# A two-block kernel: x also loaded transposed, weight units laid out in order of use, recurrence gates issued sooner, values with tokens on partitions, and the last norm's gain on VectorE

## The chip, the cores and the metric

The kernel runs on one core of a Trainium2 chip. The metric is device time of one execution in microseconds. Engines are named as the profile does: PE is TensorE's matmuls, PEld its weight loads, DVE is VectorE, ACT ScalarE, POOL GpSimd, SP SyncE. SPq and ACTq are the queues in which SyncE and ScalarE issue DMAs.

## The reference, cut to what matters

Two blocks follow one another on x of 512 tokens by 1024 features, in float32.

```
# first block
h = rmsnorm(x, norm1_g);  p = h @ w_in                    # 1024 -> 512 lru_x | 512 lru_gate | 512 four_in
c = centred_depthwise_conv(lru_x, conv_w, conv_b)         # width 4 along tokens
for direction in (forward, backward):
    r, i = sigmoid(c @ w_a + b_a), sigmoid(c @ w_x + b_x) # blocks of 64 x 64
    a = exp(8 r log_sigmoid(lam));  h_t = a h_{t-1} + sqrt(1 - a^2) (i c)
x = x + concat(gelu(lru_gate) * (h_f + h_b), fourier_mix(four_in)) @ w_out
x = x + expert_choice_moe(rmsnorm(x, norm2_g))            # 16 experts, 64 tokens each, 1024 -> 2048 -> 1024
x = rmsnorm(x, normf_g)
# second block
q, k, v, z_a, u, z_s, g_a, g_s = split(rms_norm(x, norm_gain) @ w_in_2)
y_a = (band_attention(q, k, v, rel_bias) * silu(z_a)) @ w_attn_out      # 8 heads; rel_bias by distance
y_s = gelu(s5_ssm(u));  y_s = glu(y_s @ w_glu) * silu(z_s) @ w_ssm_out  # complex state space, 32 groups
x = x + (sigmoid(g_a) * y_a + sigmoid(g_s) * y_s) @ w_out_2
return rms_norm(x, final_gain)
```

## The kernel before

Every engine executes the instructions in the order in which the program issues them to it; nothing reorders them. The tile framework adds the waits between engines. A buffer of a pool is used again once its last readers are done.

**Precision.** Matmuls of the two blocks run on a pair of a rounded part and a rest: `Pair.put` copies the rounded part on ScalarE (L106, or L109 with a scale) and subtracts it on VectorE or GpSimd (L107, L110), and `mm3` does three matmuls for a product (L120 to L122), so a unit of eight feature blocks is 24 matmuls of 128x512.

**Weights.** `Stream` loads units of 128x1024 floats (512 KB) on SyncE's queue into two buffers of two units each, `work` splits a unit and issues the next load, and `get` hands out a split unit and keeps about two ahead. A unit of w_in is 128 columns of it, read in pieces of 128 floats for each row of the matrix. Of three splits one subtracts on VectorE and two on GpSimd.

**Head.** Four blocks of 128 tokens of x are loaded (L253), transposed on TensorE into eight PSUM banks (L319) and split into `hT` with the norm's gain (L324). The squares for the norm run on ScalarE (L283), and the log-sigmoid chain of the recurrences runs on VectorE (L294 to L315). Two units are projected as hT arrives; `inv_sqrt` (L218 to L229), four scaled identities and one matmul make `rr`, the norm's scale of each token in every partition (L349). Four projections feed the convolution: for each block b one multiplication by rr (L373), one scaled copy on ScalarE (L374), three steps on VectorE (L378), and a split. `gates(b)` does the four gate products of a block with four sigmoids on ScalarE (L366); block 0's stand in the loop at b == 3, after the work on the third block. Then come the fourier projections (L426 to L432), the decays (`decay`, L398 to L401) and recurrences (`recur`, L405 to L411), pumped in between the gelu projections, the channel and token products of the Fourier mix (L453 to L476), and the output projection.

**Middle.** Router and expert choice, then 16 experts whose weights stream through two rings of buffers on SyncE's queue (`prefetch`, L201). The tables of the state space are made beside them.

**Second block.** `proj` projects one unit, tokens along the free dimension. After the queries and keys and the chunk scans of the state space come the four units of the values: `values(b)` projects 128 value columns and multiplies them by rr (L1280), and `turn_values(b)` transposes them by four matmuls (L1286) and copies them into `vt`, tokens on partitions (L1287). They stand in this order: values 0, chunk outputs 0 to 2 (L1262, L1263), turn 0, values 1, chunk outputs 3, the four turned outputs (L1271, copied into `Yc`, L1272), turn 1; then the write of Yc to DRAM (L1309), the load of the bias table `bt` on ScalarE's queue into the buffer of `U`, which the chunk outputs read (L1312), a subtraction and a fill of it on GpSimd (L1313, L1314), a fill of the two key tiles `kl` on GpSimd (L1319), and the split of head 0; then values 2, values 3, turn 2, the score matmuls of head 0 (L1370, and L1371, which reads `kl`), and turn 3. From there `fill` places 24 projections among the eight heads.

**Tail.** After the last output projection each half of a token block gets the residual (L1520), a square on ScalarE (L1523) and a multiplication by the gain on GpSimd, the very last half on VectorE (L1524); `finish` makes the scale in small VectorE steps (L218 to L229) and applies it half on ScalarE, half on VectorE (L1500, L1503).

Of the kernel before, what the change touches and what calls it, by code (L numbers as in the profile page):

```python
# [16 lines left out]
OP = mybir.AluOpType  # L17
# [35 lines left out]

NRING = 3
# [5 lines left out]
def body(ctx, tc, a, out, dbg=None):  # L60
# [63 lines left out]
    class Stream:  # L124
# [6 lines left out]
        def load(self, n=1):  # L131
            for _ in range(n):
                if self.units:
                    if self.half is None:
                        pair = wr.tile([128, 2, 1024], F32, name="w", tag="w")
                        t, self.half = pair[:, 0], pair[:, 1]
                    else:
                        t, self.half = self.half, None
                    for src, shape, *sub in self.units.pop(0):
                        v = t.rearrange(shape[0], **shape[1]) if shape else t  # L140
                        SP.dma_start(v[:, :, sub[0], :] if sub else v, src)
                    self.loaded.append(t)
# [18 lines left out]

    def cols_unit(w, c0, k=DB, width=128):

        return [(w[:, c0:c0 + width].rearrange("(k p) c -> p k c", p=128), ("p (k c) -> p k c", {"k": k}))]

    def rows_unit(w, k):
        return [(w[k * 128:(k + 1) * 128, :], None)]
# [68 lines left out]
    with ExitStack() as c1:  # L236
# [5 lines left out]
        with ExitStack() as ca:  # L242
# [5 lines left out]
            ws = Stream([cols_unit(a["w_in"], b * 128) for b in (0, 1, 2, 3, 8, 9, 10, 11, 4, 5, 6, 7)] +  # L248
                        [rows_unit(a["w_out"], k) for k in (4, 5, 6, 7, 0, 1, 2, 3)])
            for tb in range(TB):  # L250
                if tb == TB - 1:
                    ws.load()
                SP.dma_start(xs[:, tb, :], a["x"][tb * 128:(tb + 1) * 128, :])  # L253
                if tb == 0:
                    SP.dma_start(cst, a["cst"][:, 0:CCK])
                    SP.dma_start(pp, a["pp"])
            ws.load(3)
# [12 lines left out]
            ps = [bank() for _ in range(DB)]  # L270
# [11 lines left out]
            def squares(tb):  # L282
                act(h2n[:, tb, :], xs[:, tb, :], AF.Square, accum_out=ss[:, tb:tb + 1])  # L283
# [33 lines left out]
            for tb in range(TB):  # L317
                for d in range(DB):
                    PE.transpose(ps[d][:, tb * 128:(tb + 1) * 128], xs[:, tb, d * 128:(d + 1) * 128], ident)  # L319
                if 0 < tb < TB - 1:  # L320
                    squares(tb)
            ws.work(DVE)
            for d in range(DB):
                hT.put((slice(None), d), ps[d], DVE, scale=P("n1", d, d + 1))  # L324
                if d == 1:
                    ws.work(POOL)
            squares(TB - 1)
# [9 lines left out]

            w = [ws.done.pop(0) for _ in range(2)]
            two = [bank(), bank()]
            for k, i in [(k, i) for j in (range(3), range(3, DB)) for i in range(2) for k in j]:  # L340
                mm3(two[i], w[i][:, k * 128:(k + 1) * 128], hT[:, k, :], start=(k == 0), stop=(k == DB - 1))
            inv_sqrt(ta, ss, "n1", rt)
            dg = early2[:, 1]
            for tb in range(TB):
                DVE.tensor_scalar(dg[:, tb * 128:(tb + 1) * 128], ident, rt[:, tb:tb + 1], None, op0=OP.mult)
# [4 lines left out]

            two.append(in_proj())

# [18 lines left out]
            for b in range(5):  # L371
                if b < 4:
# [61 lines left out]
            fourier(0, pf)  # L434
# [5 lines left out]
            for g in range(1, 4):  # L440
                fourier(g, in_proj())
# [425 lines left out]
    order = [4, 0, 1, 2, 3, 5, 6, 7, 8, 9]  # L867
    units = [cols_unit(a["w_in_2"], g * 512 + b * 128) for g in order for b in range(4)]
    units += [cols_unit(a["w_attn_out_2"], b * 256, 4, 256) for b in range(4)]
    for b in range(4):  # L870
        units.append([(a["w_glu_2"][:, j * 512 + b * 128:j * 512 + b * 128 + 128].rearrange("(k p) c -> p k c", p=128),
                       ("p (k j c) -> p k j c", {"k": 4, "j": 2}), j) for j in range(2)])
    units += [cols_unit(a["w_ssm_out_2"], b * 256, 4, 256) for b in range(4)]
    units += [rows_unit(a["w_out_2"], k) for k in range(DB)]
    ws = Stream(units)
# [399 lines left out]
    vT = {}  # L1275

    def values(b):
        p = proj()
        vT[b] = scratch("vT")
        DVE.tensor_tensor(vT[b], p, rr, op=OP.mult)  # L1280

    def turn_values(b):
        t = vT.pop(b)
        p = bank()
        for tb in range(TB):
            PE.transpose(p[:, tb * 128:(tb + 1) * 128], t[:, tb * 128:(tb + 1) * 128], ident)  # L1286
        act(vt[:, :, b * 128:(b + 1) * 128], p.rearrange("p (t c) -> p t c", t=TB), AF.Copy)  # L1287
# [45 lines left out]
    values(2)  # L1333
    values(3)
    turn_values(2)
# [287 lines left out]
```

## Time and profile before

| | us |
|---|---|
| median of 3 runs (1524.46 to 1530.74) | 1527.55 |
| profiled execution | 1526.82 |
| its span, first to last instruction | 1525.0 |
| TensorE matmuls busy in the span | 1458.1 (96%) |
| VectorE, ScalarE, GpSimd busy | 609.8, 401.3, 192.2 |
| HBM read | 453.16 MB |

The profile is of one execution. Times in its rows count from the first instruction. An instruction's row gives its start, how long it was busy, engine and line, what it writes and reads, and in square brackets how long its engine was idle before it and which instruction or DMA ended that. Matmuls overlap, so the distance between two starts tells more than a duration.

### The profile page before, as it was taken

To read this page: it belongs to the slowest core of one execution; us is meant where nothing else is said; L and a number is where in the kernel's file an instruction comes from. 1 tells how busy PE (TensorE), PEld (TensorE's weight loads), DVE (VectorE), ACT (ScalarE), POOL (GpSimd) and SP (SyncE) were. 2 spreads that over 40 slices of the span, in tenths; PEclk is the share of its full clock that TensorE was granted. 3 is DMA by queue.
4 is the path that set the end of the run, shared out by engine and by line. 5 is a ranking of instruction groups with operands and counts; after the bars stand their busy time and mean duration, and the time that the engine had idled before them with its cause. 6 is when DMAs were issued, how large, how long until landed. Compare 5 with 4: busy or idle time off the path is not lost.

```text
span 1525.0 us, 17325 instructions
## 1 busy us (share of the span) xinstructions
PE 1458.1 (96%) x6856; PEld 807.0 (53%) x6856; DVE 609.8 (40%) x1278; ACT 401.3 (26%) x688; POOL 192.2 (13%) x128
## 2 busy tenths in 40 slices
PE   8899899999999999999999999899999899999997
PEld 6678633333333334443334343343478787777885
DVE  6773512221222244333342323442253745554454
ACT  5744211100100210100100100111173156664533
POOL 3423000000001000000000001000022232212353
PEclk9999899999999999999999999999999999999999
DMA  6116979999999999999999999999947152223331
GB/s 223 56 55 272 372 326 411 427 427 425 427 426 411 425 425 427 428 426 426 427 426 425 427 427 422 396 420 427 387 126 139 56 138 63 76 83 105 99 114 55
DMA packets 141345, 459.67 MB, mean 301 GB/s; under 512 B 16654, under 2 KB 87694, under 8 KB 93008
## 3 DMA queue, kind: packets, MB, share of 16 engines
q1 hardware_dynamic: 138848, 454.23, 74.8%
q10 hardware_dynamic: 1760, 2.62, 0.5%
q0 software_dynamic: 656, 1.71, 0.4%
q8 instruction: 54, 0.88, 0.2%
q14 instruction: 27, 0.22, 0.0%
HBM read 453.16 MB, written 4.19 MB: 300 GB/s over the span
## 4 chain that ended last, share of the span: by engine, by line
PE 78%; DMA 9%; DVE 6%; ACT 3%; issue 2%; POOL 1%; SPq 0%; ACTq 0%; POOLq 0%; DVEq 0%
PE gu L1058 25%; PE dn L1081 13%; DMA w<-in_w_up_dram 8%; PE ps L122 8%; PE ps L120 8%; PE ps L121 8%; PE tp L920 4%; PE tp L956 3%; PE tp L1045 2%; PE dn L1104 1%; DVE cT L378 1%; PE tp L945 1%; PE ps L1406 1%; ACT sh L1038 1%; PE ps L1394 1%
## 5 line engine op out<-in xcount | busy, mean ns | idle before, releaser
L1058 PE MATMUL gu<-w,xT 128*64 128x512 f32 x2032 | 472.0, 598 | 11.4 <-DMA w<-in_w_up_dram 10.6
L1058 PEld LDWEIGHTS gu<-w,xT 128*64 128x64 f32 x2032 | 167.7, 137 | 279.0 <-issue 228.6
L1081 PE MATMUL dn<-w,sh 128*64 128x512 f32 x944 | 218.0, 599 | 0.0
L958 DVE TENSOR_TENSOR xs<-tp,xs 128x512 f32<-128x512 f32 x120 | 77.5, 686 | 279.3 <-PE tp L956 279.3
L120 PE MATMUL ps<-hTh,w 128*128 128x512 f32 x416 | 167.2, 402 | 2.3 <-DVE early L475 1.5
L122 PE MATMUL ps<-hTh,w 128*128 128x512 f32 x416 | 165.2, 397 | 0.6 <-POOL w L107 0.6
L121 PE MATMUL ps<-hTl,w 128*128 128x512 f32 x416 | 165.1, 397 | 0.2 <-DVE hTl L110 0.2
L107 POOL TENSOR_TENSOR w<-w 128x1024 fp32r<-128x1024 f32 x51 | 124.1, 2436 | 279.1 <-ACT w L106 266.5
L1081 PEld LDWEIGHTS dn<-w,sh 128*64 128x64 f32 x944 | 63.9, 137 | 116.0 <-issue 115.3
L1038 ACT ACTIVATE sh<-gu 128x512 f32<-128x512 f32 x32 | 19.1, 597 | 396.1 <-PE gu L1058 393.8
L106 ACT ACTIVATE w<-w 128x1024 fp32r<-128x1024 f32 x80 | 83.7, 1054 | 64.6 <-PE ps L122 41.3
L120 PEld LDWEIGHTS ps<-hTh,w 128*128 128x128 f32 x416 | 78.9, 190 | 22.1 <-issue 3.5
L122 PEld LDWEIGHTS ps<-hTh,w 128*128 128x128 f32 x416 | 78.8, 189 | 19.7 <-POOL w L107 1.3
L121 PEld LDWEIGHTS ps<-hTl,w 128*128 128x128 f32 x416 | 78.8, 189 | 18.6 <-DVE hTl L110 0.6
L956 PE MATMUL tp<-Y,GT 128*128 128x512 f32 x240 | 72.3, 421 | 0.4 <-ACT ssm_BM L838 0.4
L956 PEld LDWEIGHTS tp<-Y,GT 128*128 128x128 f32 x240 | 40.1, 188 | 52.0 <-issue 44.6
L1040 DVE COPY sh<-gu 128x512 f32<-128x512 f32 x32 | 22.1, 690 | 103.8 <-PE gu L1058 69.6
L107 DVE TENSOR_TENSOR w<-w 128x1024 fp32r<-128x1024 f32 x29 | 41.8, 1445 | 51.8 <-ACT w L106 51.8
L849 POOL DMA_DIRECT2D ssm_BM<-raw x8 | 4.2, 536 | 459.5 <-DVE raw L845 459.5
L925 ACT ACTIVATE xin<-tp 128x512 f32<-128x512 f32 x16 | 9.6, 597 | 189.7 <-PE tp L920 189.7
L931 DVE TENSOR_TENSOR xT<-tp,pp 128x512 f32<-128x512 f32 x16 | 11.1, 692 | 117.6 <-PE tp L929 117.6
L1045 PE MATMUL tp<-cst,sh 128*128 128x128 f32 x256 | 39.1, 287 | 17.4 <-DVE sh L1053 11.7
(446 smaller groups left out, 1726.9 us busy)
## 6 DMA issues: line engine op xcount, KB each, us to landing
w<-in_w_gate_dram SPq DMA_DIRECT2D x127, 1024.0 KB, 13.3
w<-in_w_up_dram SPq DMA_DIRECT2D x127, 1024.0 KB, 14.3
w<-in_w_down_dram SPq DMA_DIRECT2D x118, 1024.0 KB, 14.7
w<-in_w_in_dram SPq DMA_DIRECT2D x52, 512.0 KB, 4.8
w<-in_w_out_dram SPq DMA_DIRECT2D x16, 512.0 KB, 4.3
w<-in_w_down_dram SPq DMA_DIRECT2D x16, 512.0 KB, 8.0
xs<-in_x_dram SPq DMA_DIRECT2D x4, 512.0 KB, 5.5
h2n<-in_w_down_dram SPq DMA_DIRECT2D x2, 1024.0 KB, 19.0
```

Of the source, the lines that this page charges most:

```text
L106: act(h, src, AF.Copy)
L107: eng.tensor_tensor(l, src, h.bitcast(F32), op=OP.subtract)
L120: PE.matmul(p, x[0], y[0], start=start, stop=False)
L121: PE.matmul(p, x[0], y[1], start=False, stop=False)
L122: PE.matmul(p, x[1], y[0], start=False, stop=stop)
L920: PE.matmul(p[h * 64:h * 64 + 64], G[:, tb, :], src[:, tb, h * 512:(h + 1) * 512], start=(tb == 0), stop=(tb == TB - 1))
L956: PE.matmul(p, GT[e][:, tb * 128:(tb + 1) * 128], Yt[e][h * 512, 512][i], start=(i == 0), stop=(i == 1))
L958: DVE.tensor_add(sl, p, sl)
L1038: act(o, i, AF.Copy)
L1045: PE.transpose(p[:, j * 128:(j + 1) * 128], gus[n][:, j * 128:(j + 1) * 128], ident)
L1058: PE.matmul(gu[n][j * 64:j * 64 + 64], xt[:, d, :], wt[kind, e, d][:, n * 512:(n + 1) * 512], start=(d == 0), stop=(d == DB - 1))
L1081: PE.matmul(dn[n][j * 64:j * 64 + 64], hTe[:, k + 8 * j, :], w[:, j * 1024 + n * 512:j * 1024 + n * 512 + 512], start=(k == 0), stop=(k == 7))
```

## The change

All matrices of the two `Stream`s are laid out on the host as stacked units in order of use, so that a unit is one load of 4 KB for each partition. x is also passed transposed; `xT0`, in the buffer of h2n, takes the transposes' place, and the warm-up matmuls are twelve. The first two units are split in halves among the parts of hT. The third unit's split and the log-sigmoid chain follow, then the squares. The gates of block 0 are issued at the start of b == 3, and one more fourier projection at its end. The values are projected with hT as the stationary operand into four banks that stay open over four units of two feature blocks each, and leave them with the norm's scale on ScalarE. The gain multiplications of the last two token blocks are on VectorE.

```diff
-            ws = Stream([cols_unit(a["w_in"], b * 128) for b in (0, 1, 2, 3, 8, 9, 10, 11, 4, 5, 6, 7)] +
-                        [rows_unit(a["w_out"], k) for k in (4, 5, 6, 7, 0, 1, 2, 3)])
+            ws = Stream([a["w1"][i] for i in range(N1)])
+            xT0 = h2n.rearrange("p t (d s) -> p (t d) s", s=S)
+            ACT.dma_start(pp, a["pp"])
+            SP.dma_start(xT0[:, 0], a["xT"][:, 0])
+            ws.load()
+            SP.dma_start(xT0[:, 1], a["xT"][:, 1])
+            ws.load()
+            for d in range(2, DB, 2):
+                SP.dma_start(xT0[:, d:d + 2], a["xT"][:, d:d + 2])
             for tb in range(TB):
-                if tb == TB - 1:
+                SP.dma_start(xs[:, tb, :], a["x"][tb * 128:(tb + 1) * 128, :])
+                if tb == 1:
                     ws.load()
...
-            for _ in range(5):
-                PE.matmul(ps[0][:, 0:128], ones, ones, start=True, stop=True)
-            squares(0)
+            p = bank()
+            for _ in range(12):
+                PE.matmul(p[:, 0:128], ones, ones, start=True, stop=True)
...
+            def half(i, j, eng):
+                u, t = w[i]
+                u.put((slice(None), slice(j * 512, j * 512 + 512)), t[:, j * 512:j * 512 + 512], eng)
+            def part(d):
+                hT.put((slice(None), d), xT0[:, d], DVE, scale=P("n1", d, d + 1))
+            half(0, 0, DVE)
+            part(0)
+            part(1)
+            half(1, 0, DVE)
+            part(2)
+            half(0, 1, POOL)
+            part(3)
+            half(1, 1, POOL)
+            for d in range(4, DB):
+                part(d)
...
+            two = [bank(), bank()]
+            for k, i in [(k, i) for j in (range(2), range(2, 4), range(4, DB)) for i in range(2) for k in j]:
+                mm3(two[i], w[i][:, k * 128:(k + 1) * 128], hT[:, k, :], start=(k == 0), stop=(k == DB - 1))
+            ws.load(2)
+            ws.work(DVE)
...
             for tb in range(TB):
-                for d in range(DB):
-                    PE.transpose(ps[d][:, tb * 128:(tb + 1) * 128], xs[:, tb, d * 128:(d + 1) * 128], ident)
...
+                act(early[:, 0:2].rearrange("p a b -> p (a b)"), xs[:, tb, :], AF.Square, accum_out=ss[:, tb:tb + 1])
+            inv_sqrt(ta, ss, "n1", rt)
...
             ws.work(POOL)
...
+            two.append(in_proj())
             pr = bank()
             PE.matmul(pr, ones, dg, start=True, stop=True)
             rr = early2[:, 0]
             act(rr, pr, AF.Copy)
-            two.append(in_proj())
...
             for b in range(5):
+                if b == 3:
+                    gates(0)
...
                 if b == 2:
-                    pf = in_proj()
+                    pf = [in_proj()]
                 if b == 3:
-                    gates(0)
+                    pf.append(in_proj())
...
-                fourier(g, in_proj())
+                fourier(g, pf[1] if g == 1 else in_proj())
...
+    ws = Stream([a["w2"][i] for i in range(N2)])
...
+    vp = []
+    def values(i):
+        if i == 0:
+            vp.extend(bank() for _ in range(TB))
+        w = ws.get()
+        for k in range(2):
+            for tb in range(TB):
+                mm3(vp[tb], hT[:, 2 * i + k, tb * 128:(tb + 1) * 128], w[:, k * 512:(k + 1) * 512],
+                    start=(i == 0 and k == 0), stop=(i == 3 and k == 1))
...
     for q in range(3):
         chunk_outputs(q)
-    turn_values(0)
     values(1)
+    values(2)
     Yc = stile("cos", [128, 32, 64], "Yc")
     chunk_outputs(3)
+    values(3)
     for q in range(4):
         turn_outputs(q)
-    turn_values(1)
+    for tb in range(TB):
+        act(vt[:, tb, :], vp[tb], AF.Copy, scale=stat[:, 7, tb:tb + 1])
...
     split_head(0)
-    values(2)
-    values(3)
-    turn_values(2)
...
-            if h == 0:
-                turn_values(3)
...
-            (DVE if tb == TB - 1 and h else POOL).tensor_tensor(jk[:, tb, c], sl, fg[:, c], op=OP.mult)
+            (DVE if tb > 1 else POOL).tensor_tensor(jk[:, tb, c], sl, fg[:, c], op=OP.mult)
```

## Rows read from the trace of the kernel before

**Rows 1.** Page, part 4: the chain that ended last, by engine.

```profile
PE 78%; DMA 9%; DVE 6%; ACT 3%; issue 2%; POOL 1%; SPq 0%; ACTq 0%; POOLq 0%; DVEq 0%
```

**Rows 2.** Page, part 2: DMA busy, tenths, in 40 slices of 38 us.

```profile
DMA  6116979999999999999999999999947152223331
```

**Rows 3.** Timeline, SyncE's queue, 62 to 200 us: start, us, what.

```profile
168.53 0.33 SPq L201 DMA_DIRECT2D w<-in_w_up_dram  x1
```

**Rows 4.** Windows: us, busy us (instructions) by engine, granted clock, DMA share, GB/s.

```profile
62.00:80.00 18.00, 18.00 (x78) 14.48 (x78) 9.71 (x12) 17.23 (x25) 11.50 (x13) 1.00 0.20 58
...
100.00:120.00 20.00, 18.51 (x72) 14.10 (x71) 16.93 (x26) 4.76 (x9) 2.40 (x1) 0.91 0.15 53
...
1320.00:1400.00 80.00, 80.00 (x393) 63.52 (x390) 41.95 (x100) 50.43 (x87) 19.18 (x8) 1.00 0.24 74
```

**Rows 5.** Timeline, TensorE, 0 to 113 us; idle before in brackets.

```profile
4.74 1.94 PE L319 MATMUL ps<-cst,xs 128*128 128x128 f32 x8 [1.21 <-DMA cst<-in_cst_dram]
...
13.21 0.50 PE L120 MATMUL ps<-hTh,w 128*128 128x512 f32 x1 [0.80 <-DVE hTl L110]
...
53.41 0.80 PE L120 MATMUL ps<-cs,mixFh 128*128 128x512 f32 x1 [5.34 <-ACT h2n L366]
...
111.65 0.49 PE L120 MATMUL ps<-hTh,w 128*128 128x512 f32 x1 [1.49 <-DVE early L475]
```

**Rows 6.** DMA rate in 40 slices of 1.5 us, 0 to 60 us.

```profile
GB/s 0 259 307 293 364 326 408 344 347 356 449 419 398 338 331 20 11 0 0 0 16 241 346 96 0 5 0 0 81 336 282 0 0 0 5 0 0 0 0 11
```

**Rows 7.** Timeline, ScalarE, 24 to 92 us.

```profile
26.22 0.60 ACT L349 ACTIVATE early<-ps 128x512 f32<-128x512 f32 x1 [6.78 <-PE ps L347]
...
83.25 1.05 ACT L106 ACTIVATE w<-w 128x1024 fp32r<-128x1024 f32 x1
...
85.77 0.60 ACT L457 ACTIVATE abf<-ps 128x512 f32<-128x512 f32 x1 [1.48 <-PE ps L453]
...
89.35 1.28 ACT L405 ACT_TABLE_LOAD   x1
```

**Rows 8.** Timeline, VectorE, 0 to 66 us.

```profile
5.47 0.17 DVE L294 COPY l_in<-pp 128x4 f32<-128x4 f32 x1 [5.47 <-DMA pp<-in_pp_dram]
...
11.09 0.16 DVE L315 TENSOR_SCALAR ls<-ls 128x8 f32<-128x8 f32 x1
...
18.47 0.16 DVE L218 TENSOR_SCALAR v_n<-ss 128x4 f32<-128x4 f32 x1
...
29.52 6.94 DVE L378 SCALAR_TENSOR_TENSOR cT<-uT,pp,cT 128x512 f32<-128x512 f32 x3 [1.38 <-ACT cT L374]
...
52.00 2.32 DVE L378 SCALAR_TENSOR_TENSOR cT<-uT,pp,cT 128x512 f32<-128x512 f32 x3
```

**Rows 9.** Timeline, TensorE, 1198 to 1250 us.

```profile
1226.92 0.60 PE L1286 MATMUL ps<-cst,vT 128*128 128x128 f32 x4
...
1227.27 0.48 PE L120 MATMUL ps<-hTh,w 128*128 128x512 f32 x1
...
1238.51 0.60 PE L1286 MATMUL ps<-cst,vT 128*128 128x128 f32 x4
...
1239.06 0.28 PE L1371 MATMUL ps<-att 128*128 128x256 f32 x1
```

**Rows 10.** Timeline, ScalarE's DMA queue, 1185 to 1260 us.

```profile
1227.56 0.42 ACTq L1312 DMA_DIRECT2D bt<-in_rel_dram  x1
```

**Rows 11.** Chain of waits, 1195 to 1245 us: start, us, what.

```profile
1225.82 2.07 ACT Yc L1272 x4
...
1234.11 3.60 POOL bt L1313
...
1241.84 0.50 PE ps L122
```

**Rows 12.** Timeline, VectorE, 1490 us to the end.

```profile
1515.57 1.25 DVE L225 SCALAR_TENSOR_TENSOR t_r<-y_r,v_r 128x1 f32<-128x1 f32 x1
...
1519.72 0.22 DVE L225 SCALAR_TENSOR_TENSOR t_r<-y_r,v_r 128x1 f32<-128x1 f32 x1
```

More of the change, by code (lines that the diff above doesn't have):

```diff
@@ L138, in load @@
                         t, self.half = self.half, None
-                    for src, shape, *sub in self.units.pop(0):
-                        v = t.rearrange(shape[0], **shape[1]) if shape else t
-                        SP.dma_start(v[:, :, sub[0], :] if sub else v, src)
+                    SP.dma_start(t, self.units.pop(0))
                     self.loaded.append(t)
@@ L317, in body @@
             for tb in range(TB):
-                for d in range(DB):
-                    PE.transpose(ps[d][:, tb * 128:(tb + 1) * 128], xs[:, tb, d * 128:(d + 1) * 128], ident)
[L320 to L327, printed above, removed]
+                act(early[:, 0:2].rearrange("p a b -> p (a b)"), xs[:, tb, :], AF.Square, accum_out=ss[:, tb:tb + 1])
+            inv_sqrt(ta, ss, "n1", rt)
+            dg = early2[:, 1]
+            for tb in range(TB):
+                DVE.tensor_scalar(dg[:, tb * 128:(tb + 1) * 128], ident, rt[:, tb:tb + 1], None, op0=OP.mult)
             ws.work(POOL)
@@ L335, in in_proj @@
                 return p
[L338 to L345, printed above, removed]
+            two.append(in_proj())
             pr = bank()
@@ L432, in fourier @@
                 POOL.tensor_copy(fm[:, g:g + 1], fT[:, g, 256:257])
[L434 removed]
+            fourier(0, pf[0])
             for b in range(4):
@@ L1592, in layout, with unit @@
     g = {"cst": constants(), "pp": pp, "lru_bd": bd.reshape(128, 2048), "x": x["x"][0]}
-    for n in ("w_in", "w_out", "w_gate", "w_up", "w_down"):
+    g["xT"] = x["x"][0].T.reshape(DB, 128, S).transpose(1, 0, 2)
+    for n in ("w_gate", "w_up", "w_down"):
         g[n] = x[n]
-    for n in ("w_in_2", "w_glu_2", "w_attn_out_2", "w_ssm_out_2", "w_out_2"):
-        g[n] = x[n][0]
+    def unit(w, k0, k, c0, c):
+        return w[k0 * 128:(k0 + k) * 128, c0:c0 + c].reshape(k, 128, c).transpose(1, 0, 2).reshape(128, 1024)
+    w = x["w_in"]
+    g["w1"] = np.stack([unit(w, 0, DB, b * 128, 128) for b in (0, 1, 2, 3, 8, 9, 10, 11, 4, 5, 6, 7)] +
+                       [unit(x["w_out"], k, 1, 0, D) for k in (4, 5, 6, 7, 0, 1, 2, 3)])
+    w, u = x["w_in_2"][0], []
+    for c in (4, 0, 1, 2, 3, 5, 6, 7, 8, 9):
+        for b in range(4):
+            u.append(unit(w, 2 * b, 2, c * 512, 512) if c == 2 else unit(w, 0, DB, c * 512 + b * 128, 128))
+    u += [unit(x["w_attn_out_2"][0], 0, 4, b * 256, 256) for b in range(4)]
+    w = x["w_glu_2"][0].reshape(512, 2, 512)
+    u += [unit(w[:, :, b * 128:b * 128 + 128].reshape(512, 256), 0, 4, 0, 256) for b in range(4)]
+    u += [unit(x["w_ssm_out_2"][0], 0, 4, b * 256, 256) for b in range(4)]
+    u += [unit(x["w_out_2"][0], k, 1, 0, D) for k in range(DB)]
+    g["w2"] = np.stack(u)
     for n in ("normf_g", "final_gain_2"):
```

43 lines of the change are left out of this document (11 added, 32 removed).

## The prediction

> **What bounds the kernel now.** I read the chain of waits first [rows 1]: TensorE holds 78% of it, DMA 9%, VectorE 6%, ScalarE 3%. The kernel is a TensorE kernel with a few places where something else sets the pace, so the question for each edit is whether it touches such a place. The slices [rows 2] show the middle: from the seventh slice to the twenty-ninth the DMA engines are busy 9 tenths or more, where the expert weights stream in. The change edits nothing there. But time won before it arrives at the end: the queue that carries the stream halts and goes on at 168.53 us [rows 3], behind the last units of the first output projection, so stream and TensorE move together and I count a microsecond won before that as one at the end. After the experts TensorE is full: 80.00 of 80 us at granted clock 1.00 from 1320 to 1400 [rows 4]. Nothing there can give back what is lost at 1200.
>
> In the head TensorE starts its first projection at 13.21 us, after the transposes of x that begin at 4.74. It then stops twice: 5.34 us up to 53.41, ended by ScalarE's sigmoids, and 1.49 us up to 111.65, ended by VectorE [rows 5]. Between them ScalarE is the full engine, 17.23 of 18 us from 62 to 80 [rows 4].
>
> **x also loaded transposed.** The 32 transposes and their wait go. What replaces them is 2 MB more to load. The first block of x was on chip at 4.74 [rows 5]; block 0 of xT and the first half unit, 0.75 MB, are about as much as had come by 6.5 us ([rows 6]; an estimate), so TensorE can start 6.7 us sooner. If TensorE alone set the pace, this, the 5.34 us stop and the half clock behind such a stop would go: 6.7 + 5.3 + 1.8 = 13.8 us. The 1.8 us is the window from 100 to 120, whose clock of 0.91 [rows 4] behind the stop of 1.49 us is 0.09 x 20 us lost. That is the upper bound.
>
> What is late next is the row of scales rr, which every block of the convolution needs. It was copied by 26.82 [rows 7]. The change queues VectorE differently: the log-sigmoid chain, which ran from 5.47 to 11.25 [rows 8] while x was still loading, now stands behind the parts of hT and behind the split of the third unit. That unit is behind 4.9 MB (2.1 of xT, 1.0 of two units, 1.0 of two x blocks, 0.5 its own, 0.2 of parameters). The rate averaged 353 GB/s from 1.5 to 22.5 us and reached 449 [rows 6]; at 353 the unit lands at 15.4, at 427 at 13.0; I take 14.2. Copy 1.05 [rows 7], the subtraction I take as long, chain 5.8: 22.1. The norm's steps from L218 at 18.47 [rows 8] to the end of rr took 8.35 before; the hard part of that is no more than half, the rest is queues on TensorE and GpSimd. I take 6: rr at 28.1, 1.3 later than before (bounds 25 and 32). Two weight copies of 1.05 that ScalarE ran between rr and the first convolution now stand ahead of rr, which gives back 1.1 of the 2.70 us from 26.82 to 29.52. So the convolution starts at 29.7, 0.2 later.
>
> One rule bears on that landing: the Trainium skill, page "DMA: Bandwidth & Descriptors", section "Specifications", has 512 bytes as the least transfer for line rate; the old units are read in pieces of just that, so by the rule their new layout wins nothing and 353 GB/s stays: the unit lands at 15.4 and the sum below ends 1.2 us later, at 1535.2. The rate of [rows 6], which rises to 449 as the larger rows follow, speaks for some gain, and I stay between.
>
> **Weight units in order of use.** Behind the head, loads run two or more units ahead; they are hidden by the 5.62 us that TensorE takes for a unit ((1238.51 - 1227.27) / 2 [rows 9]). Zero; if the cover were gone, one landing of some microseconds once, and none of the stops in [rows 5] was ended by a unit's load.
>
> **Gates sooner, a fourier projection more.** Three convolution steps took 6.94 us for block 0 and 2.32 for block 3 [rows 8]: the 4.62 more are GpSimd subtractions running beside, about two. In block 0 one of these is now over before it begins, -2.3 (bounds 0 and -4.6). But the projection added at b == 3 splits one more unit on GpSimd, beside block 3, which ran free: +2.3 (bounds 0 and 2.4). They cancel, and the end of the convolution, 54.32 [rows 8], moves by +0.2. From there ScalarE works without a wait to 84.30; it then waits for TensorE's channel products, idle in 84.30 to 89.35 but for three copies of 0.60: 3.3 us [rows 7]. With one projection done early, TensorE comes to the channels 5.6 us sooner and this wait goes; one weight copy of 1.05 is also done before. -3.3 - 1.1 = -4.4. The stop at 111.65 stays, since VectorE's recurrences, which end it, follow ScalarE's square roots. The four sigmoids issued before the third convolution block delay its copy on ScalarE only, while VectorE still works on the block before: zero, or up to 1 us if that cover is short. Head: +0.2 - 4.4 = -4.2, bounds -9 and +1 (-13.8 is a rival).
>
> **Values with tokens on partitions.** The matmuls stay 24 a unit. Sixteen transposes go, 0.35 us for four (1226.92 to 1227.27 [rows 9]), and four VectorE multiplications, which were on no path. What is moved matters more. Before, units 2 and 3 of the values stand behind the turned outputs, and these 11.24 us cover a chain: the copies into Yc, the load of bt on ScalarE's queue (issued 1227.56 [rows 10]), GpSimd's subtraction from 1234.11 for 3.60, two fills of bt and of the key tile, and only then the score matmul L1371 at 1239.06 [rows 9, 11]. It fits almost exactly: the chain that ended last runs through these steps and reaches TensorE, which waits, at 1241.84 [rows 11]. Now all four units stand ahead of the turned outputs, nothing of TensorE's stands between these and the scores, and on ScalarE the load of bt waits behind the Yc and value copies; GpSimd's fills wait behind bt, and the scores for the fills. The start of the chain moves later by 2 x 5.62 less four transposes, 0.35: 10.9 us, and TensorE idles for the 11.5 us from issue to L1371. Saved behind the scores: four transposes, 0.35, and the last wait, about 0.6, as that unit's split now stands ahead of bt. Added: half clock after an idle time that long, 1.8 as above. 10.9 - 0.35 - 0.6 + 1.8 = +11.7. Bounds: +8, if bt lands 2 us sooner and the clock costs nothing, and +14, if the load waits until the four value copies have run, as long as the Yc copies, 2.07 [rows 11].
>
> **Last norm on VectorE.** One small VectorE step took 1.25 us beside GpSimd and 0.22 without [rows 12]. For the last two token blocks such delays go, about 1.0 each, and three multiplications of half a block come to VectorE. Nearly even: -0.3, bounds -1 and +1.
>
> **Sum.** The profiled execution took 1526.82, its span 1525.0 and 1.8 around it; the median shown is 1527.55. 1526.8 - 4.2 + 11.7 - 0.3 = 1534.0, which is 6.4 us or 0.4% over the median. 0.5% (7.6 us, so 1519.9 and 1535.2) is about what a measurement can tell from no change.
>
> **Rivals.**
> *The head gives nothing* (slower): rr waits on VectorE's queue longer than I take, 3 us and more, and the convolution and everything ScalarE does behind it slide by the 4.4 won. For it: VectorE's in-order queue now holds the wait for the third unit ahead of all of the chain. Against: ScalarE's weight copies are out of the way. 1526.8 + 11.7 - 0.3 = 1538.2; it is slower by over 0.5% from a head gain under 3 us.
> *TensorE sets the pace in the head*: the convolution runs free of GpSimd and all 13.8 us arrive. For it: the stops in [rows 5]; against: ScalarE's full windows. 1526.8 - 13.8 + 11.7 - 0.3 = 1524.4.
> *The bt chain stays covered* (not slower): if bt were issued some 11 us before the turned outputs end, TensorE would lose nothing and win 4 x 0.35 + 0.6 = 2.0. For it: the old U tile is free by then but for the last chunk; against: ScalarE's queue reaches the load only past copies that need the turned outputs. 1526.8 - 4.2 - 2.0 - 0.3 = 1520.3. It decides from a wait under 5 us.
>
> **How the numbers follow.** Forecast 0.45, head gives nothing 0.25, TensorE's pace 0.14, bt covered 0.16. The likeliest is 1534, by itself 1529 to 1538 from its bounds. Of the forecast's 0.45 I put 0.17 over 1535.2; of the second case 0.24; so slower 0.41. Faster: 0.03 of TensorE's pace, 0.09 of bt covered, 0.12. Same: 0.47. The range that leaves out one in ten on each side goes from within the bt case to the head case with its upper bounds: 1521 to 1541.
>
> **What would show it.** Right: TensorE idle 10 us or more before the first score matmul, ended by GpSimd's fill; bt's load issued after the turned outputs; the first recurrence multiplication about 4 us sooner; the copy of rr at 26 to 30 us. Wrong: rr before 24 us, a convolution block 0 near 2.3 us, TensorE's stop before the gates gone and the first expert more than 8 us sooner; or scores without a stop.

## The result

The changed kernel takes 1537.47 us, the median of 5 runs (1536.05 to 1540.04). The kernel before, run beside it, takes 1529.38 (1524.46 to 1530.74). The ratio is 1.0062, with an interval of 1.0041 to 1.0083: 9.5 us slower by the ratio, which is that of the means, and 8.1 by the medians. With 0.5% as the bound it is slower, though the interval reaches a little below that. The forecast was 1534.0, in a range from 1521 to 1541. The range held. By its own bound of 0.5% the forecast had given 0.47 to no change, 0.41 to slower and 0.12 to faster. In absolute time the result lies 0.7 us from that of the first rival, "the head gives nothing", 1538.2. But both sums start from the profiled execution of 1526.8. As differences the forecast is +7.2 and the rival +11.4, and the measured 8.1 to 9.5 lie between them, so the time alone doesn't tell them apart.

Below, a ratio of r is told as (r - 1) x 1529 us, so that runs beside different executions of the kernel before can be compared. The half widths of these intervals are 1.5 to 3.2 us, and a difference between two such figures carries both.

### The profile after

The profiled execution took 1536.9 us, its span 1535.1. First TensorE's timeline in the head: start and duration in us, engine, line, operation; idle before and what ended it in brackets.

```profile
7.53 0.51 PE L121 MATMUL ps<-hTh,w 128*128 128x512 f32 x1 [1.82 <-ACT hTh L110]
...
31.44 2.07 PE L360 MATMUL ps<-early 128*128 128x512 f32 x2 [4.86 <-DVE early L348]
...
61.87 0.50 PE L121 MATMUL ps<-cs,mixFh 128*128 128x512 f32 x1 [3.64 <-ACT h2n L376]
...
113.22 0.47 PE L121 MATMUL ps<-hTh,w 128*128 128x512 f32 x1 [1.50 <-DVE early L487]
```

The first projection begins 5.7 us sooner than in [rows 5], the two old stops come later (61.87 and 113.22), and there is a new one: 4.86 us before the matmul that makes rr, ended by VectorE's identities. VectorE's timeline of the same stretch shows why.

```profile
17.97 0.16 DVE L320 COPY l_in<-pp 128x4 f32<-128x4 f32 x1
...
23.60 0.17 DVE L341 TENSOR_SCALAR ls<-ls 128x8 f32<-128x8 f32 x1
24.83 0.17 DVE L210 TENSOR_SCALAR v_n<-ss 128x4 f32<-128x4 f32 x1 [1.06 <-ACT early L344]
...
26.28 5.11 DVE L348 TENSOR_SCALAR early<-cst,rt 128x128 f32<-128x128 f32 x4
...
36.25 4.44 DVE L390 SCALAR_TENSOR_TENSOR cT<-uT,pp,cT 128x512 f32<-128x512 f32 x3 [0.78 <-ACT cT L386]
...
46.43 2.31 DVE L390 SCALAR_TENSOR_TENSOR cT<-uT,pp,cT 128x512 f32<-128x512 f32 x3
...
56.27 4.31 DVE L390 SCALAR_TENSOR_TENSOR cT<-uT,pp,cT 128x512 f32<-128x512 f32 x3
```

GpSimd begins two splits with the first identity:

```profile
26.27 4.64 POOL L108 TENSOR_TENSOR w<-w 128x1024 fp32r<-128x1024 f32 x2 [12.52 <-DVE rt L221]
```

The log-sigmoid chain stands at 17.97 to 23.77, where [rows 8] had it at 5.47. Behind it VectorE waits once more, for ScalarE's sums of squares, and then four identities take 5.11 us. Block 0 of the convolution (36.25) is 2.5 us shorter than in [rows 8], block 3 (56.27) 2.0 longer, as forecast. ScalarE's timeline:

```profile
15.74 1.06 ACT L107 ACTIVATE w<-w 128x1024 fp32r<-128x1024 f32 x1 [1.52 <-DMA w<-in_w_dram]
18.24 0.21 ACT L323 ACTIVATE ey<-l_in 128x8 f32<-128x8 f32 x1 [1.44 <-DVE l_in L321]
...
20.12 1.04 ACT L344 ACTIVATE early<-xs 128x1024 f32<-128x1024 f32 x1
...
33.55 0.60 ACT L362 ACTIVATE early<-ps 128x512 f32<-128x512 f32 x1 [6.01 <-PE ps L360]
...
90.30 0.59 ACT L474 ACTIVATE al<-ps 1x512 f32<-1x512 f32 x1 [0.59 <-PE ps L473]
90.91 1.28 ACT L417 ACT_TABLE_LOAD   x1
```

rr is copied by 34.15, not by 26.82 as in [rows 7], but the square roots begin only 1.56 us later than there: 56.8 us after rr instead of 62.5. The wait for the channels is down to 0.59 us. SyncE's queue goes on with the expert stream 1.57 us later than in [rows 3]:

```profile
170.10 0.33 SPq L193 DMA_DIRECT2D w<-in_w_up_dram  x1
```

The DMA rate over the first 60 us, in slices of 1.5 us as in [rows 6], is higher and has a later end, for 2 MB more:

```profile
GB/s 0 143 342 407 414 423 415 426 421 415 418 404 454 417 415 415 377 60 3 27 317 355 0 0 5 0 0 0 0 0 0 134 415 150 0 0 0 5 0 0
```

Now the scores. TensorE, 1228 to 1262 us:

```profile
1235.81 1.91 PE L1275 MATMUL ps<-cst,y 128*128 128x128 f32 x16
1242.57 0.58 PE L1371 MATMUL ps<-att 128*128 128x256 f32 x1 [4.86 <-ACT att L1333]
1249.44 0.58 PE L1372 MATMUL ps<-att 128*128 128x256 f32 x1 [6.28 <-POOL att L1323]
```

ScalarE and its queue, and GpSimd, in the same stretch:

```profile
1237.76 0.39 ACTq L1316 DMA_DIRECT2D bt<-in_rel_dram  x1
...
1238.43 2.45 ACT L1311 ACTIVATE vt<-ps,stat 128x512 f32<-128x512 f32 x4
...
1241.89 0.63 ACT L1333 ACTIVATE att<-qk 64x512 fp32r<-64x512 f32 x1
```

```profile
1244.63 3.60 POOL L1317 TENSOR_TENSOR bt<-bt,bfar 128x2048 f32<-128x2048 f32 x1 [18.28 <-DMA bt<-in_rel_dram]
1248.29 0.52 POOL L1318 MEMSET bt<- 64x512 f32 x1
1248.86 1.09 POOL L1323 MEMSET att<- 64x512 f32 x2
```

This is the chain of [rows 9 to 11], and it is bare. The load of bt is issued 10.2 us later than in [rows 10]; TensorE has nothing left after the turned outputs and stands 11.1 us in two stops, the first ended by ScalarE's split of the first head, the second by GpSimd's fill of the key tile, which waits behind bt's subtraction. The windows of that stretch (columns as in [rows 4]) show the price of the clock as well: from 1241 to 1254 TensorE is busy 5.15 of 13 us, at granted clock 0.50.

```profile
1228.00:1241.00 13.00, 9.71 (x74) 8.03 (x72) 1.23 (x1) 6.04 (x11) 0.00 (x0) 0.97 0.40 112
1241.00:1254.00 13.00, 5.15 (x14) 4.18 (x15) 5.11 (x14) 4.68 (x11) 5.16 (x4) 0.50 0.54 132
```

### The profile page after: what moved, and what is told of

It is laid out like the page before. It is cut to its first block, busy times and chain, and to the rows that moved or that the text cites. A ratio compares the mean times of both kernels' runs of the same rounds, so it can differ in the third digit from the quotient of the medians.

```text
span 1535.1 us, 17258 instructions
## 1 busy us (share of the span) xinstructions
PE 1457.6 (95%) x6822; PEld 805.3 (52%) x6822; DVE 607.4 (40%) x1279; ACT 403.1 (26%) x690; POOL 184.0 (12%) x125
## 5 line engine op out<-in xcount | busy, mean ns | idle before, releaser
L121 PE MATMUL ps<-hTh,w 128*128 128x512 f32 x384 | 156.1, 406 | 3.3 <-ACT hTh L110 1.8
L108 POOL TENSOR_TENSOR w<-w 128x1024 fp32r<-128x1024 f32 (+1 forms) x51 | 121.9, 2395 | 283.1 <-ACT w L107 247.8
L122 PE MATMUL ps<-hTl,w 128*128 128x512 f32 x384 | 153.8, 400 | 0.3 <-DVE hTl L111 0.3
L123 PE MATMUL ps<-hTh,w 128*128 128x512 f32 x384 | 153.2, 399 | 0.0
L107 ACT ACTIVATE w<-w 128x1024 fp32r<-128x1024 f32 (+1 forms) x82 | 84.1, 1032 | 73.9 <-PE ps L123 43.5
L121 PEld LDWEIGHTS ps<-hTh,w 128*128 128x128 f32 x384 | 73.4, 191 | 22.5 <-issue 3.8
L122 PEld LDWEIGHTS ps<-hTl,w 128*128 128x128 f32 x384 | 73.7, 192 | 17.9 <-DVE hTl L111 0.6
L123 PEld LDWEIGHTS ps<-hTh,w 128*128 128x128 f32 x384 | 73.7, 192 | 17.6
L108 DVE TENSOR_TENSOR w<-w 128x1024 fp32r<-128x1024 f32 (+1 forms) x31 | 39.5, 1277 | 73.4 <-ACT w L107 73.4
L1044 DVE COPY sh<-gu 128x512 f32<-128x512 f32 x32 | 22.1, 691 | 105.6 <-PE gu L1062 71.5
L935 DVE TENSOR_TENSOR xT<-tp,pp 128x512 f32<-128x512 f32 x16 | 11.1, 692 | 118.2 <-PE tp L933 118.2
L1049 PE MATMUL tp<-cst,sh 128*128 128x128 f32 x256 | 38.9, 285 | 17.0 <-DVE sh L1057 11.5
```

The source lines that it names most:

```text
L107: act(h, src, AF.Copy)
L108: eng.tensor_tensor(l, src, h.bitcast(F32), op=OP.subtract)
L121: PE.matmul(p, x[0], y[0], start=start, stop=False)
L122: PE.matmul(p, x[0], y[1], start=False, stop=False)
L123: PE.matmul(p, x[1], y[0], start=False, stop=stop)
L1044: DVE.tensor_copy(o, i)
```

## The experiments

### Which half lost the time

Old values in the changed kernel:

```diff
...
+    turn_values(0)
     values(1)
-    values(2)
     Yc = stile("cos", [128, 32, 64], "Yc")
     chunk_outputs(3)
-    values(3)
     for q in range(4):
         turn_outputs(q)
-    for tb in range(TB):
-        act(vt[:, tb, :], vp[tb], AF.Copy, scale=stat[:, 7, tb:tb + 1])
+    turn_values(1)
...
     split_head(0)
+    values(2)
+    values(3)
+    turn_values(2)
...
+            if h == 0:
+                turn_values(3)
```

> The changed kernel with the values as before it: turned by transposes, units 2 and 3 behind the first split of a head, their four weight units laid out by columns again; head, other weight units and last norm stay changed. If the loss is the chain of bt (my account), TensorE has no stop over 1 us between the turned outputs and the first scores and the time is that of the kernel before plus what the head is worth at its end, between -1 and +2 us. If the head lost the time (the rival: rr 7 us later, carried to the end), the kernel stays 5 us or more above the kernel before.

Measured: 1528.38 us, ratio 1.0001 (0.9990 to 1.0013), so +0.2 us. Between the turned outputs and the scores TensorE has no stop. The four weight units of the values are laid out for the old products here.

The reverse, new values alone in the kernel before:

```diff
...
-    turn_values(0)
     values(1)
+    values(2)
     Yc = stile("cos", [128, 32, 64], "Yc")
     chunk_outputs(3)
+    values(3)
     for q in range(4):
         turn_outputs(q)
-    turn_values(1)
+    for tb in range(TB):
+        act(vt[:, tb, :], vp[tb], AF.Copy, scale=stat[:, 7, tb:tb + 1])
...
     split_head(0)
-    values(2)
-    values(3)
-    turn_values(2)
...
-            if h == 0:
-                turn_values(3)
```

> The kernel before with the new values alone (their four weight units laid out for it). If the bt chain is the loss: +9 to +11 us, with about 11 us of TensorE stops ahead of the first scores. If the head is the loss: under +4. If the parts add up, this run's difference and that of the run with the old values sum to the changed kernel's +8.

Measured: 1539.86, ratio 1.0079 (1.0061 to 1.0097), +12.1 us, a little over the 9 to 11 expected, with two stops ahead of the scores:

```profile
1244.78 0.58 PE L1367 MATMUL ps<-att 128*128 128x256 f32 x1 [4.85 <-ACT att L1329]
1251.34 0.58 PE L1368 MATMUL ps<-att 128*128 128x256 f32 x1 [5.98 <-POOL att L1319]
```

The new values, where they stand, are the whole loss; head, layout and tail together are worth nothing, within 2 us. The sum, 12.1 + 0.2, agrees with the 9.5 of the change within the intervals.

### Which step of the chain

The key tile's fills ahead of bt's subtraction, bt's load where it was:

```diff
-    POOL.tensor_tensor(bt, bt, bfar[:, :, None].to_broadcast([128, 8, 256]), op=OP.subtract)
-    POOL.memset(bt[0:64, :, 0:64], -1e30)
...
     for i in range(2):
         POOL.memset(kl[i][(1 - i) * 64:(1 - i) * 64 + 64].bitcast(F32), 0.0)
...
+    POOL.tensor_tensor(bt, bt, bfar[:, :, None].to_broadcast([128, 8, 256]), op=OP.subtract)
+    POOL.memset(bt[0:64, :, 0:64], -1e30)
```

> The changed kernel with one move in GpSimd's queue: the two fills of the key tile are issued ahead of bt's subtraction and fill, which still wait for the same load. If the scores wait only for these fills (queue order), the second stop, 6.28 us ended by GpSimd, goes, the first of 4.86 ended by ScalarE's copies stays, and the time falls by 5 to 6 us. If the scores' next steps need bt as badly (the rival: the load itself is the bound), the stop moves behind the score matmuls and the time falls by under 2 us.

Measured: 1530.53, ratio 1.0022 (1.0009 to 1.0034), 6.1 us less than the change. TensorE and GpSimd of this run:

```profile
1245.19 0.58 PE L1371 MATMUL ps<-att 128*128 128x256 f32 x1 [4.85 <-ACT att L1333]
1245.57 0.53 PE L1372 MATMUL ps<-att 128*128 128x256 f32 x1
```

```profile
1232.93 1.09 POOL L1320 MEMSET att<- 64x512 f32 x2 [3.97 <-issue]
1247.26 3.60 POOL L1322 TENSOR_TENSOR bt<-bt,bfar 128x2048 f32<-128x2048 f32 x1 [13.24 <-DMA bt<-in_rel_dram]
```

The fills run at 1232.93, the second stop is gone, the first stands as it was. bt arrives as late as before and nobody on TensorE misses it: the 6.28 us were the order of GpSimd's queue and not the load of bt.

All of the preparations ahead of the last unit of the values:

```diff
     chunk_outputs(3)
...
+    ACT.dma_start(bt, bass.AP(tensor=a["rel"].tensor, offset=a["rel"].offset, ap=[[1, 128], [384, 8], [1, 256]]))
...
+    for i in range(2):
+        POOL.memset(kl[i][(1 - i) * 64:(1 - i) * 64 + 64].bitcast(F32), 0.0)
...
+    POOL.tensor_tensor(bt, bt, bfar[:, :, None].to_broadcast([128, 8, 256]), op=OP.subtract)
+    POOL.memset(bt[0:64, :, 0:64], -1e30)
...
+    split_head(0)
...
     values(3)
     for q in range(4):
         turn_outputs(q)
...
```

The same lines are gone from their old place behind the turned outputs.

> The changed kernel with bt's load, the fills of the key tile ahead of bt's subtraction, and the first split of a head all issued ahead of the fourth unit of the values and of the turned outputs. If the whole loss there is a matter of order, both stops go (11.1 us) and the half clock behind them: the time falls by 9 to 12 us and ends 1 to 4 us below the kernel before. If the turned outputs' copies or the value copies, now later on ScalarE, bind instead, a stop of 3 us or more shows at the transposes of the turned outputs or at the first use of the values, and the gain is under 7 us.

Measured: 1524.27, ratio 0.9978 (0.9965 to 0.9990), 12.9 us less than the change, a little over the 9 to 12 expected, and 3.4 less than the kernel before. TensorE goes from the turned outputs into the scores without a stop:

```profile
1239.75 1.91 PE L1275 MATMUL ps<-cst,y 128*128 128x128 f32 x16
1241.42 0.36 PE L1371 MATMUL ps<-att 128*128 128x256 f32 x1
1241.62 0.28 PE L1372 MATMUL ps<-att 128*128 128x256 f32 x1
```

So the new values are not slow in themselves: with the chain covered they are 3.6 us better than the old ones (-3.4 against +0.2).

### Why rr was late

The two weight splits from GpSimd to VectorE, behind the identities:

```diff
-            ws.work(POOL)
+            ws.work(DVE)
+            ws.work(DVE)
```

> The changed kernel with one edit in the head: the third and fourth further weight units are split by VectorE, behind the four scaled identities, and not by GpSimd beside them. If GpSimd's splits are what stretches the identities (5.11 us instead of 0.88), they take about 0.9 us, rr is ready about 4 us sooner (at 30 instead of 34), and the square roots on ScalarE start 3 to 4 us sooner, at about 87. If the pace there is another (TensorE's third unit, the queue of VectorE), rr comes under 1.5 us sooner. At the end 2 to 4 us less if the head arrives there, nothing if it is swallowed on the way.

Measured: 1534.94, ratio 1.0030 (1.0018 to 1.0043), 4.9 us less than the change. The identities are those of the kernel before, rr is there at 28.72 and the square roots begin at 86.44:

```profile
26.03 0.87 DVE L348 TENSOR_SCALAR early<-cst,rt 128x128 f32<-128x128 f32 x4
```

```profile
26.96 1.13 PE L361 MATMUL ps<-early 128*128 128x512 f32 x2 [1.21 <-DVE early L348]
```

```profile
28.12 0.60 ACT L363 ACTIVATE early<-ps 128x512 f32<-128x512 f32 x1 [0.63 <-PE ps L361]
...
86.44 1.28 ACT L418 ACT_TABLE_LOAD   x1
```

Of the 5.4 us that rr wins, 4.2 are the identities; another 0.9 is TensorE's, which makes rr in 1.13 us here, at granted clock 1.00 from 26 to 28 us, and took 2.07 behind the stop of 4.86, at granted clock 0.50 from 31.40 to 33.50. The Trainium skill, page "SBUF — State Buffer", section "Who interferes with whom", has VectorE and GpSimd share a pair of ports: an instruction that takes the pair holds it to its end, the other engine waits for all of it, and `tensor_scalar`, the identities' operation, is among those that can take it. The trace agrees with such a wait: the identities are 4.24 us longer beside 4.64 us of GpSimd.

The trace of the kernel before shows the like on the way to rr, at another step. There the identities ran free, and a small step of the norm stood beside a split:

```profile
19.68 2.16 DVE L225 TENSOR_TENSOR t_n<-rt 128x4 f32<-128x4 f32 x1
...
22.47 0.88 DVE L345 TENSOR_SCALAR early<-cst,rt 128x128 f32<-128x128 f32 x4
```

```profile
19.42 2.39 POOL L107 TENSOR_TENSOR w<-w 128x1024 fp32r<-128x1024 f32 x1 [3.06 <-ACT w L106]
```

In the change that step (L217) takes 0.16 us.

The log-sigmoid chain out of the way, GpSimd as in the change:

```diff
...
+            DVE.tensor_copy(l_in[:, 0:4], P("lamf"))
+            DVE.tensor_copy(l_in[:, 4:8], P("lamb"))
...
+            act(ey, l_in, AF.Abs)
+            act(ey, ey, AF.Exp, scale=-1.0)
...
             half(0, 0, DVE)
...
             ws.work(DVE)
...
-            DVE.tensor_copy(l_in[:, 0:4], P("lamf"))
...
-            DVE.tensor_scalar(ls2, ls, 2.0, None, op0=OP.mult)
             act(rt, rt, AF.Sqrt)
...
+            DVE.tensor_scalar(sv, ey, 2.0, None, op0=OP.add)
...
+            DVE.tensor_scalar(ls2, ls, 2.0, None, op0=OP.mult)
             def decay(dr, b):
...
```

> The changed kernel with the log-sigmoid chain taken out of rr's way: its two copies and ScalarE's two steps stand ahead of the parts of hT, the rest of it behind the convolution; GpSimd's splits stay. If VectorE's order made rr late (the chain behind the third unit's split), the square sums start about 2 us sooner and rr comes 2 us sooner, with the identities still near 5 us. If the chain was hidden by ScalarE's squares and rr waits for something else, rr moves by under 0.7 us.

Measured: 1533.95, ratio 1.0032 (1.0016 to 1.0048), 4.6 us less. The identities begin 2.0 us sooner, as expected, but rr comes 5.0 us sooner, at 29.13, and not 2. VectorE, the copy of rr and GpSimd show why:

```profile
24.28 3.03 DVE L332 TENSOR_SCALAR early<-cst,rt 128x128 f32<-128x128 f32 x4
```

```profile
28.53 0.60 ACT L346 ACTIVATE early<-ps 128x512 f32<-128x512 f32 x1 [0.55 <-PE ps L344]
```

```profile
24.26 2.38 POOL L108 TENSOR_TENSOR w<-w 128x1024 fp32r<-128x1024 f32 x1 [10.63 <-DVE rt L221]
28.06 2.40 POOL L108 TENSOR_TENSOR w<-w 128x1024 fp32r<-128x1024 f32 x1 [1.42 <-ACT w L107]
```

Two microseconds earlier, the identities meet one split instead of two; the second one's copy on ScalarE still waits for its load (2.74 us, up to 26.93). The expectation of a length near 5 us was wrong; both reasons were at work.

Both edits, the chain's only by its last line:

```diff
...
-            DVE.tensor_scalar(ls2, ls, 2.0, None, op0=OP.mult)
             act(rt, rt, AF.Sqrt)
...
-            ws.work(POOL)
+            ws.work(DVE)
+            ws.work(DVE)
...
+            DVE.tensor_scalar(ls2, ls, 2.0, None, op0=OP.mult)
             def decay(dr, b):
```

> Both edits of the head together: no GpSimd split beside the identities, and the log-sigmoid chain out of the way. My account: rr at about 28 instead of 34, so what I had forecast for it; the square roots start at about 85.5 and the first expert 4 to 6 us sooner, and the time falls by 3 to 6 us against the changed kernel. Rival: the convolution or the recurrences take it back, the square roots start later than 88.5, and the time falls by under 2 us.

Measured: 1534.29, ratio 1.0030 (1.0020 to 1.0039), 4.9 us less, no more than each alone. rr is there at 27.99 and the square roots begin at 85.74, as expected; the first expert's first turned tile comes at 220.5 instead of 225.0 (223.5 to 227.8 in the profiles with the change's head). The first multiplication of the recurrences stands at 87.70, against 91.31 in the kernel before. Each edit alone had already brought rr within about a microsecond of this.

### Two terms that the forecast had named

The gates of block 0 behind the third block again, one projection instead of two:

```diff
-                if b == 3:
-                    gates(0)
...
                 if b == 3:
-                    pf.append(in_proj())
+                    gates(0)
...
-                fourier(g, pf[1] if g == 1 else in_proj())
+                fourier(g, in_proj())
```

> The changed kernel with the gates of block 0 again behind the third convolution block and one fourier projection instead of two issued in the convolution. By the terms of the forecast the stretch from the end of rr's copy to the square roots (56.8 us in the changed kernel's trace) loses the 4.4 us won on ScalarE and wins 2.3 in block 3, which runs free of GpSimd again: about 59. If the gates and the projection are what shortened this stretch by more than that (62.5 before), it comes to 61 or more; if they did nothing, it stays under 57.5. The time moves by 0 to 3 us, which is near what three rounds can tell.

Measured: 1541.76, ratio 1.0081 (1.0060 to 1.0101), 2.9 us over the change, which lies inside the two intervals. VectorE's block 3 and ScalarE's square roots:

```profile
55.97 2.32 DVE L388 SCALAR_TENSOR_TENSOR cT<-uT,pp,cT 128x512 f32<-128x512 f32 x3
```

```profile
93.02 1.28 ACT L415 ACT_TABLE_LOAD   x1
```

From the end of rr's copy, 33.89, to 93.02 it is 59.1 us, against 56.8 in the change: the two terms ask for 58.9. In the other profiles with the change's head this stretch is 56.6 to 57.8, so agreement this close is in part luck; the run does show that it grows by about the terms and doesn't come near 61.

The first projection's units by columns, in pieces of 512 bytes:

```diff
-            ws = Stream([a["w1"][i] for i in range(N1)])
+            ws = Stream([a["w_in"][:, b * 128:b * 128 + 128].rearrange("(k p) c -> p k c", p=128)
+                         for b in (0, 1, 2, 3, 8, 9, 10, 11, 4, 5, 6, 7)] + [a["w1"][i] for i in range(12, N1)])
...
```

> The changed kernel with the twelve units of the first projection loaded by columns, in pieces of 512 bytes, as before; the rest unchanged. If the layout in order of use is what raised the rate of the head's loads (about 415 GB/s), the rate falls towards 350, the third unit lands about 2 us later than at 15.7 and rr comes 1 to 2 us later. If the layout gives nothing, the third unit lands within 0.5 us of 15.7. At the end within 2 us in either case.

Measured: 1539.05, ratio 1.0065 (1.0047 to 1.0084), 0.5 us over the change. The third unit's copy on ScalarE:

```profile
16.09 1.06 ACT L107 ACTIVATE w<-w 128x1024 fp32r<-128x1024 f32 x1 [1.64 <-DMA w<-in_w_in_dram]
```

0.35 us later than in the change, and rr 0.34: at the landing the layout gives next to nothing. The rate does rise while a unit moves. From 11.05 to 14.65 us the kernel before moves only packets under 2 KB, at 347 GB/s; from 13.75 to 15.55 this run, with 992 of 1030 packets under 2 KB, moves 363 and the change 421. But the third unit is 0.5 MB of some 5.4 that have come when it is there (summed from the slices of the profile after).

### Versions that beat both kernels

Both edits of the head, and the scores' preparations ahead, each shown by one or two of its lines:

```diff
...
-            ws.work(POOL)
+            ws.work(DVE)
+            ws.work(DVE)
...
     chunk_outputs(3)
...
+    split_head(0)
...
     values(3)
...
```

> Both edits of the head and the scores' preparations ahead of the fourth unit of the values. If the two losses are apart, the gains add: 13 us for the one and 3 to 6 for the other, so 1518 to 1522, 7 to 11 us below the kernel before. If the head's gain doesn't reach the end, the time is that of the preparations alone, about 1524.

Measured: 1519.76, ratio 0.9942 (0.9928 to 0.9955), 8.9 us less than the kernel before. The head's edits are worth 5.5 us here (half width 2.8), so they arrive at the end.

The same, and the four GpSimd splits beside the convolution given to VectorE:

```diff
-                    bds.put((slice(None), slice(b * 1024, b * 1024 + 1024)), bd[:, b * 1024:b * 1024 + 1024], POOL)
+                    bds.put((slice(None), slice(b * 1024, b * 1024 + 1024)), bd[:, b * 1024:b * 1024 + 1024], DVE)
...
-                    pf = [in_proj()]
+                    pf = [in_proj(DVE)]
...
-                    pf.append(in_proj())
+                    pf.append(in_proj(DVE))
...
```

> The kernel with both edits of the head and the scores' preparations ahead, and now also the four GpSimd splits that run beside the convolution (two of the recurrence's block weights, two of weight units) done by VectorE. If a GpSimd split costs a convolution block about 2 us, three blocks fall from 4.3 to 2.3, VectorE takes 1.2 us for each split instead, and the square roots start 3 to 5 us sooner; the end 2 to 5 us below that kernel's 1519.8. If VectorE was not the engine that binds the convolution, or its own splits take as much as they free, under 1 us.

Measured: 1516.18, ratio 0.9917 (0.9901 to 0.9933), 3.8 us less again, with a half width of 3.2. The square roots begin at 83.55 instead of 86.01, 2.5 us sooner and not the 3 to 5 expected. A split takes VectorE 1.23 us and every convolution block takes 2.32. The last pair:

```profile
49.70 1.23 DVE L108 TENSOR_TENSOR w<-w 128x1024 fp32r<-128x1024 f32 x1 [0.25 <-ACT w L107]
50.85 2.32 DVE L377 SCALAR_TENSOR_TENSOR cT<-uT,pp,cT 128x512 f32<-128x512 f32 x3
```

And the second unit of the values ahead of the chunk outputs:

```diff
     values(0)
+    values(1)
     chunk_states(3)
     for q in range(3):
         chunk_outputs(q)
-    values(1)
     values(2)
```

> The same, and the second unit of the values issued ahead of the first chunk outputs, where TensorE stops for 4.9 us until VectorE has the states ready. If that stop is a matter of order too, it goes, and the time falls by another 4 to 5 us. If the weights of that unit aren't ready sooner, or the later steps wait for the outputs that come later, part of it shows as a stop behind it.

Measured: 1512.11, ratio 0.9885 (0.9865 to 0.9906), 17.6 us less than the kernel before and 4.9 less than without this move, with a half width of 4.0. TensorE's stop at the chunk outputs, which the kernel before has too (4.83 us), without the move and with it:

```profile
1203.02 0.47 PE L1270 MATMUL ps<-ssm_W,Hs 128*64 128x128 f32 x1 [4.87 <-DVE Hs L1257]
```

```profile
1210.24 0.32 PE L1270 MATMUL ps<-ssm_W,Hs 128*64 128x128 f32 x1 [1.43 <-DVE Hs L1257]
```

Behind it TensorE has no other stop up to the end of the first scores.

## Why the prediction was right or wrong, step by step

**Values and the chain of bt: right.** Forecast +11.7, bounds 8 to 14. Measured +12.1 alone in the kernel before, and 9.3 between the change and the change with old values. The stops add up to 11.1 us against the 11.5 forecast, and the order of the steps is the one that was told, GpSimd's fills behind bt and the scores behind the fills. One detail was not named: the first stop, 4.86 us, is ScalarE's, whose copies to vt stand ahead of the split of the first head. The forecast's 2.0 us of gain for a covered chain was 3.6 (half width 2.6).

**The head: the step that failed is "I take 6: rr at 28.1, 1.3 later than before (bounds 25 and 32)".** rr came at 34.15, outside the bounds. Up to the end of the log-sigmoid chain the account was 1.7 us short (23.77 for 22.1), most of it the landing of the third unit (15.7 for 14.2). From there it took 10.4 us and not 6. Two causes, both tested: the identities ran beside two GpSimd splits that the change itself had moved there (4.2 us), and the matmul behind them ran at half clock (0.9). In the run without GpSimd beside the identities the same stretch takes 5.2 us, inside the 6. The forecast called the rest of the 8.35 us "queues on TensorE and GpSimd" and supposed that they would be mostly empty. The trace of the kernel before had the price: 2.0 of the 8.35 us were one norm step beside a split. The forecast even counted a GpSimd split that would be over before block 0 of the convolution, and took 2.3 us off there; it never asked what that split would then run beside. Nor was the chain on VectorE the last to end: the sums of squares on ScalarE were (VectorE waits 1.06 us for them up to 24.83), because they too stood behind a step that waits for the chain's first two copies (18.24).

**The rest of the head: right.** From rr to the square roots the terms -1.1, -2.3, +2.3 and -4.4 add up to -5.5; the traces have 62.5 and 56.8, so -5.8. Undoing the gates and the projection gave 59.1. (One reading was a little off: ScalarE does wait once before 84.30, for 0.54 us at 74.34.) With rr at 27.99, as forecast, the head is worth 4.9 us more than the changed kernel's +0.2, so -4.7 against the -4.5 forecast with the tail. The half width of that is about 4 us, so it fits a term lost through rr alone and doesn't prove it. The first rival came true at its price: head, layout and tail together give +0.2. Of its reason, VectorE's queue, only a part did: the wait for the squares behind it, 2.0 us; the longest part was GpSimd's.

**TensorE's start: near, and worth nothing, as the sum had it.** 5.7 us sooner for 6.7. The first unit's copy begins at 6.23, near the 6.5 that was put for the landing, but copies and subtractions take another 1.3 us to the first matmul, which the estimate left out. The 6.5 is no reading of [rows 6] either: by these slices 0.75 MB had come at about 4.2 us. TensorE stands 4.86 us in the new stop.

**Layout: right at zero behind the head; at the landing the forecast's 1.2 us of gain was 0.35.** The rule of the Trainium skill that the prediction weighed ("DMA: Bandwidth & Descriptors", section "Specifications") had the units' new layout win nothing. At the landing the run with pieces of 512 bytes nearly agrees, with 0.35 us; in the rate it doesn't, since such pieces moved at 347 GB/s and the change's rows at 421. That the landing, 15.7, is near the 15.4 by that rule is luck: some 5.4 MB had come by then, not 4.9, at 380 GB/s on the mean from 1.5 us (estimates from the slices).

**Last norm: right in sign.** From the first residual sum to the end of VectorE's last scaling it is 18.95 us before and 17.94 after: -1.0, at the forecast's bound. In the third token block the small step of [rows 12] takes 0.22 us now, at 1526.87.

**The sum: closer than its parts.** Forecast +7.2, measured +9.5. The values came out 2.4 us under their term by the difference to the change with old values (9.3 for 11.7), the rest 4.7 over its own (+0.2 for -4.5). That these partly cancel is luck.

**The signs.** Two came: TensorE idle over 10 us ahead of the scores, though in two stops of which GpSimd's fill ended the second, and bt's load issued after the turned outputs. Two did not: the copy of rr, and the first multiplication of the recurrences, at 92.87 and so 1.6 us later than in the kernel before instead of 4 sooner.

**Left open.** Profiles of kernels with one and the same head drift apart. In the four that share the change's head (the change, old values, key fills first, preparations ahead) the square roots begin at 90.6 to 91.9 us, the first expert's turned tile comes at 223.5 to 227.8 and the last one's at 1094.7 to 1098.5. Most of the drift is there before the first expert; from the first to the last expert they differ by 1.8 us. What sets it stays open. Because of it no single profile shows whether a few microseconds of the head arrive; the ratios do, within their intervals.

## What to carry to other kernels

Before an edit moves work ahead of something, list what that work was covering: here two units of projections were the cover of a load, a subtraction and two fills, and the whole loss was 11 us of bare chain, won back by issuing the fills and the load sooner. In a queue that runs in order, put what the next engine waits for ahead of what still waits for a load. And where a short step stands on the path, look up what GpSimd does in the same microseconds: a move that only shifts its work can make steps that take 0.9 us together take five.

## What was not expected of the hardware

Four VectorE steps with a single tensor operand and a scalar, 0.88 us together, took 5.11 beside two GpSimd splits; I had looked for this only at steps with two tensor operands, such as the convolution's, where one GpSimd subtraction of 2.4 us costs VectorE 2.0 us (4.31 against 2.32). VectorE did the same subtraction in 1.23 us, so in this head sharing the work between the two engines was slower than VectorE alone.
